# Hybrid decoder layer with 32 experts: buffers given back earlier, p @ ple_proj spread over the layer, returned rows on GpSimd's queue, sums a tile ahead

## The chip, the cores and the metric

The kernel runs on one core of one Trainium2 chip. The metric is the device time of one execution in microseconds (us), as the median of several runs. The engines in the text: TensorE (PE, with its weight loads PEld), VectorE (DVE), ScalarE (ACT), GpSimd (POOL) and SyncE (SP), of which SP here does nothing but issue DMAs. A queue is a list of DMAs that one engine issues in order: SP's runs as q1 in the profile, GpSimd's as q0.

## The reference

One decoder layer over 512 tokens of width 1024, all in float32. After the mixers (not touched here) come three steps:

```python
h = h + mix @ w_out                                        # out projection
h = h + hier_moe(rmsnorm(h, norm2_g), ...)                 # 4 groups x 8 experts, 2 experts per token
gate = sigmoid(rmsnorm(h, ple_norm_g) @ ple_gate_w + ple_gate_b)   # 1024 x 1024
e = p @ ple_proj_w                                         # 512 x 256 by 256 x 1024
h = h + gate * e
return rmsnorm(h, final_norm_g)
```

In `hier_moe` each token takes the best group and in it the best two of eight experts; an expert is `silu(t @ w_gate) * (t @ w_up)` (width 256) times its combine weight, and `@ w_down`. The reference computes all experts for all tokens; the kernel sends each expert only its own tokens.

## The kernel before, in words

**Experts by pairs.** The 32 experts run as 16 pairs. An expert has 64 slots for tokens, so a pair fills the 128 partitions. For pair i, `fetch` gathers the token rows from DRAM (xg, an indirect DMA by POOL, L934), `gather_T` transposes them on PE and scales them on DVE (two halves, L976 and L977), `gate_up` runs 32 matmuls (its records are at L988), ACT and DVE make hid (L993, L994), `down` transposes hid (L1010, L1011) and runs 8 matmuls dn (L1020, two records each, as all float32 matmuls here), ACT evicts dn (L1024), and POOL scatters the 128 rows to yd in DRAM (L1033). The rows of yd are sorted by token: two rows for each token, one for each of its experts. The last pair doesn't go through DRAM: `scatter` (L1041) multiplies its rows by one-hot matrices on PE and adds them to h1 on DVE (L1043).

**Weights and the ring.** The weights of the experts are 96 pieces of 1 MB, six for a pair: first k-half of both experts' gate and up, second k-half, then both downs (the order (0,3,1,4,2,5) in `load_units`, L689). Each lies in a buffer of 8 KB per partition, called unit. There are 20 units in a ring: `unit()` takes the first free one, `free()` puts it back. A load waits for the last reader of its unit's earlier contents, and for the landing of the load three ahead (AHEAD = 3). All these loads are on SP's queue, in the order in which the code is written; so are the gate's weights, the read-back of yd and the stores of half the result. SP waits for one load's conditions before it looks at the next.

**p @ ple_proj.** `ple_load` (L710, L711) loads pT, 0.5 MB, and pW, 1 MB, in pair 6, after gate/up(6). The product has 32 steps of one 128x256 matmul each (pe, L722); every fourth step is followed by an eviction on ACT (L725) into the tiles eo, two units taken in pair 7. The table PLE says how many steps run in pairs 8 to 14, all but one ahead of a pair's gate/up and one ahead of its down.

**The end.** After gate/up(14) the engines ACT and DVE, too, run in the written order, as PE and SP do throughout. After down(14) SP's queue has gate 0, then y0 (the read-back of the two yd rows of token tile 0, L1121, which waits for the last scatter), then gates 1 to 3, the bias row, y1 to y3 and the last norm's row. `add_y` adds the rows to h1 (L1117). The gate's weights are split into a high part (ACT, L1054) and a low part (DVE, L1057), eight splits of 128x1024. `turn` transposes h1 (L1176) and splits it; then come the products pg (L1197), three matmuls for each of eight k and each half, and `finish` with the last norm. `tail` goes through four token tiles; in the products of tile t it calls `sums(t + 1)` (add_y and scatter) and `prep(t + 1)` (turn). At the end a count tells whether an expert had more than 64 tokens; a branch that is not taken here would compute those.

**Order.** PE's and SP's instructions run in the order of the code, in the whole experts stage; ACT's and DVE's from pair 14 on.

## Time and profile before

| what | value |
|---|---|
| median of 3 runs | 562.01 us (561.25 to 562.83) |
| the profiled execution's own time | 562.7 us |
| its span | 560.9 us |
| mean granted TensorE clock | 0.97 |
| PE busy | 513.1 us, 91% of the span |
| DVE, ACT, POOL busy | 276.0, 209.8, 85.3 us |
| SP's queue q1 | 137.20 MB, 63.6% of the DMA engines' span |
| POOL's queue q0 | 7.95 MB, 3.8% |

The experts run from about 240 to 481 us of the span, the gate and the last norm from there to the end. Busy shares are means over stages with different limits, so the stages are to be read one by one: windows give each engine's busy time, the clock that the throttle granted to TensorE (1.00 is full speed) and how full the DMA engines were. A timeline row has start and length; in brackets stands how long the engine had been idle before, and what released it. A group of records can span waits that are shorter than the view's bound, so its length isn't always its busy time.

### The profile page before, as it was taken

What the parts mean: (1) busy time and instruction counts of PE and PEld (TensorE: products, weight loads), DVE (VectorE), ACT (ScalarE), POOL (GpSimd) and SP (SyncE); (2) the same over time, 40 slices, a digit from 0 to 9 for tenths busy, and PEclk for the clock granted to TensorE, in tenths of its full rate; (3) what the DMA queues carried; (4) which work ended last, traced back from release to release, by engine and by line L of the source; (5) the groups of instructions that cost most, each with busy time, mean ns of one, the idle gap of its engine ahead of it and who ended that gap; (6) DMA issues with size and microseconds to landing.
All of it is one profiled execution on the core that took longest, in us unless ns stands there. A gap on an engine that the chain in (4) does not pass through costs nothing.

```text
span 560.9 us, 7565 instructions
## 1 busy us (share of the span) xinstructions
PE 513.1 (91%) x2713; PEld 322.1 (57%) x2713; DVE 276.0 (49%) x727; ACT 209.8 (37%) x435; POOL 85.3 (15%) x122
## 2 busy tenths in 40 slices
PE   8899999999999999979999999099999999679992
PEld 5797886877997788934333333044434333347782
DVE  6663957757846666772422222022122112687774
ACT  7466765656857444211111111001111112363442
POOL 3301121311009400002111111001111100010000
PEclk9999999999999999998999999699999999899997
DMA  8882222300449579978999999999999999861111
GB/s 305 262 330 59 74 65 78 100 1 2 134 156 420 221 294 424 356 278 327 403 417 414 393 390 377 375 409 389 395 408 420 391 415 377 348 252 37 39 38 41
DMA packets 35641, 148.82 MB, mean 265 GB/s; under 512 B 6557, under 2 KB 13597, under 8 KB 22160
## 3 DMA queue, kind: packets, MB, share of 16 engines
q1 hardware_dynamic: 29984, 137.20, 63.6%
q0 software_dynamic: 4320, 7.95, 3.8%
q10 hardware_dynamic: 1296, 3.15, 1.4%
q8 instruction: 23, 0.38, 0.3%
q14 instruction: 18, 0.15, 0.1%
HBM read 139.61 MB, written 16.25 MB: 278 GB/s over the span
## 4 chain that ended last, share of the span: by engine, by line
PE 74%; DMA 10%; DVE 7%; ACT 5%; issue 2%; POOL 1%; SPq 0%; DVEq 0%; ACTq 0%; POOLq 0%
PE gu L988 17%; PE pj L232 9%; PE dn L1020 8%; PE po L78 8%; DMA unit<-in_w_exp_dram 5%; PE pj L255 5%; PE pg L1197 4%; PE z L255 4%; PE pe L722 3%; PE z L309 2%; DMA unit<-in_ple_proj_w_dram 2%; PE po L331 2%; DVE h L1117 2%; PE x L965 1%; DMA xg<-tnd,idx 1%
## 5 line engine op out<-in xcount | busy, mean ns | idle before, releaser
L988 PE MATMUL gu<-unit,xT 128*64 128x512 f32 x512 | 116.7, 597 | 0.0
L988 PEld LDWEIGHTS gu<-unit,xT 128*64 128x64 f32 x512 | 34.5, 136 | 62.3 <-issue 60.9
L1020 PE MATMUL dn<-unit,hidT 128*64 128x512 f32 x256 | 60.1, 612 | 1.0 <-ACT hidT L1011 0.5
L232 PE MATMUL pj<-xh,wp 128*128 128x512 f32 x176 | 51.2, 398 | 0.3 <-ACT wp L67 0.3
L1197 PE MATMUL pg<-unit 128*128 128x512 f32 (+1 forms) x216 | 49.4, 384 | 1.5 <-DVE unit L1057 1.5
L993 ACT ACTIVATE sg<-gu 128x256 f32<-128x256 f32 x16 | 6.1, 384 | 106.8 <-PE gu L988 106.8
L921 DVE COPY SL<-sl 128x10 f32<-128x10 f32 (+1 forms) x17 | 2.9, 168 | 85.0 <-PE sl L920 85.0
L1197 PEld LDWEIGHTS pg<-unit 128*128 128x128 f32 x216 | 37.9, 194 | 11.2 <-DVE unit L1057 3.4
L994 DVE SCALAR_TENSOR_TENSOR hid<-sg,wsl,gu 128x256 f32<-128x256 f32 x16 | 7.7, 480 | 74.4 <-ACT sg L993 74.4
L1033 POOL DMA_INDIRECT yd<-big,idy x15 | 15.1, 1009 | 150.4 <-ACT big L1024 150.4
L232 PEld LDWEIGHTS pj<-xh,wp 128*128 128x128 f32 x176 | 32.5, 188 | 8.1 <-ACT wp L67 1.2
L1020 PEld LDWEIGHTS dn<-unit,hidT 128*64 128x64 f32 x256 | 17.3, 140 | 33.6 <-issue 28.1
L1024 ACT ACTIVATE big<-dn 128x512 f32<-128x512 f32 x30 | 17.9, 597 | 49.6 <-PE dn L1020 49.6
L68 DVE TENSOR_TENSOR wp<-wraw,wp 128x768 fp32r<-128x768 f32 (+2 forms) x28 | 25.8, 928 | 13.6 <-ACT wp L67 13.4
L722 PE MATMUL pe<-unit,big 128*128 128x256 f32 x64 | 18.4, 420 | 13.4 <-DMA unit<-in_ple_proj_w_dram 13.4
L67 ACT ACTIVATE wp<-wraw 128x768 fp32r<-128x768 f32 (+2 forms) x28 | 22.8, 817 | 20.2 <-PE pj L232 9.8
L232 PE MATMUL pj<-xl,wp 128*128 128x512 f32 x88 | 29.4, 400 | 0.0
L78 PE MATMUL po<-wo,mx 128*128 128x512 f32 x96 | 25.6, 407 | 0.0
L255 PE MATMUL pj<-wp,xh 128*128 128x384 f32 x96 | 24.8, 351 | 0.0
L78 PE MATMUL po<-unit,mx 128*128 128x512 f32 x96 | 24.1, 400 | 0.0
L977 DVE TENSOR_TENSOR xT<-xt,g2c 128x512 f32<-128x512 f32 x30 | 20.6, 688 | 6.7 <-PE xt L976 6.7
L934 POOL DMA_INDIRECT xg<-tnd,idx x15 | 15.4, 1029 | 55.7 <-issue 35.7
(293 smaller groups left out, 878.8 us busy)
## 6 DMA issues: line engine op xcount, KB each, us to landing
unit<-in_w_exp_dram SPq DMA_DIRECT2D x96, 1024.0 KB, 9.2
wraw<-in_w_in_dram SPq DMA_DIRECT2D x20, 384.0 KB, 6.1
yd<-zero SPq DMA_DIRECT2D x4, 1024.0 KB
unit<-in_ple_gate_w_dram SPq DMA_DIRECT2D x4, 1024.0 KB
unit<-yd SPq DMA_DIRECT2D x4, 1024.0 KB, 4.8
wraw<-in_w_out_dram SPq DMA_DIRECT2D x8, 256.0 KB, 2.9
h<-in_x_dram SPq DMA_DIRECT2D x4, 512.0 KB, 4.1
unit<-in_w_out_dram SPq DMA_DIRECT2D x4, 512.0 KB, 7.9
```

The source lines that it names most:

```text
L67: nc.scalar.activation(h, src, AF.Copy)
L68: nc.vector.tensor_tensor(l, src, h.bitcast(F32), ALU.subtract)
L78: nc.tensor.matmul(p, a[k][:, ts_], K["wo"][k][:, b, hs], start=(n == 0), stop=(n == 3 * len(ks) - 1))
L232: PE.matmul(q, a[:, i * P:(i + 1) * P], b[k], start=(n == 0), stop=(n == 3 * KC - 1))
L255: PE.matmul(p[t][:, :W_IN[j]], a[k][:, t * P:(t + 1) * P], b, start=(n == 0), stop=(n == 3 * KC - 1))
L722: PE.matmul(p[:, c * 256:c * 256 + 256], pT[:, k * S + t * P:k * S + (t + 1) * P], pW[:, k, n:n + 256], start=(k == 0), stop=(k == 1))
L934: G.indirect_dma_start(out=xg[i % 2], out_offset=None, in_=tnd, in_offset=bass.IndirectOffsetOnAxis(ap=idx[:, i:i + 1], axis=0), bounds_ch ...
L977: V.tensor_tensor(xTs[i, hf], p.rearrange("p (a b) -> p a b", a=4), g2c[:, 4 * hf:4 * hf + 4, None].to_broadcast([P, 4, P]), ALU.mult)
L988: PE.matmul(gu[64 * e:64 * e + 64], xTs[i, k // 4][:, k % 4, 64 * e:64 * e + 64], w[e][k // 4][:, 512 * (k % 4):512 * (k % 4) + 512], star ...
L1020: PE.matmul(dn[64 * e:64 * e + 64], hT[:, f, 64 * e:64 * e + 64], w[e][2][:, 1024 * f + 512 * hf:1024 * f + 512 * hf + 512], start=(f == 0 ...
L1024: SC.activation(o[:, 512 * hf:512 * hf + 512], dn, AF.Copy)
L1197: PE.matmul(p, hT[t][:, a, ks], gw[k][:, b, hs], start=start and n == 0, stop=stop and n == len(ab) - 1)
```

## The change

- **Buffers.** In each pair the units of the first k-half (pieces 0 and 3) are put back into the ring at k == 3 of gate/up and the next loads are issued in the code there; before, all four of gate and up were put back after gate/up.
- **p @ ple_proj.** pT and pW are loaded after the first ten experts' loads that follow the router's bias. pW keeps a unit from then to the end. The steps run after gate/up of pair 0 (5), of each pair 1 to 13 (1), of 14 (2), and 4 + 4 + 4 in the end: after down(15), between `scatter` and `turn`, and after `turn`. The two tiles eo are taken in pairs 3 and 7; evictions wait in the list `kept` until their tile is there.
- **Queues.** The four read-backs y0 to y3 are issued by GpSimd (queue q0). SP's queue has the four gate loads and the two rows right behind the experts' last loads.
- **Gate.** Its weights are loaded as four pieces of 4 k by 512 columns and split by halves, 128x512: three splits of the first half ahead of add_y(0), the fourth after scatter, four after turn, then eight of the second half.
- **The end.** `sums(t + 2)` is called in the last products of tile t; before, `sums(t + 1)` in its first. The results of down(15) lie in one unit and no longer in the two big tiles. The stores are of 384 columns (ACT's queue) and 640 (SP's), before 512 and 512. The count of the tokens beyond 64 is written into pair 15 and ahead of the second half's splits.

SP's queue, from the router's bias to the end of the loads (w_exp: experts' weights; pT and ple_proj_w: the projection's inputs; yd: the scattered rows; ple_gate_w: the gate's weights), before:

```order
L702 DMA rb<-in_router_b_dram 128x36
L689 DMA unit<-in_w_exp_dram 128x2048 x47
L710 DMA big<-in_pT_dram 128x1024
L711 DMA unit<-in_ple_proj_w_dram 128x2048
L689 DMA unit<-in_w_exp_dram 128x2048 x40
L1050 DMA unit<-in_ple_gate_w_dram 128x2048
L1121 DMA unit<-yd 128x2x1024
L1050 DMA unit<-in_ple_gate_w_dram 128x2048 x3
L1151 DMA rows<-in_ple_gate_b_dram 128x1024
L1121 DMA unit<-yd 128x2x1024 x3
L1154 DMA rows<-in_final_norm_g_dram 128x1024
```

And now:

```order
L704 DMA rb<-in_router_b_dram 128x36
L691 DMA unit<-in_w_exp_dram 128x2048 x7
L712 DMA big<-in_pT_dram 128x1024
L713 DMA unit<-in_ple_proj_w_dram 128x2048
L691 DMA unit<-in_w_exp_dram 128x2048 x80
L1060 DMA unit<-in_ple_gate_w_dram 128x2048 x4
L1190 DMA rows<-in_ple_gate_b_dram 128x1024
L1191 DMA rows<-in_final_norm_g_dram 128x1024
```

pT and pW moved forty loads ahead, the four reads of yd left this queue, and the four gates follow the experts' weights without a break.

PE from down(15) on (ht and dn: down; sc: scatter; xt: turn; pg: the gate's products; pe: the projection's steps), before:

```order
L1010 MATMUL ht<-ident,hid 128x128 x2
L1020 MATMUL dn<-unit,hidT 64x512 x8
L1041 MATMUL sc<-big,xT 128x512 x4
L1176 MATMUL xt<-ident,h_0_1508 128x128 x8
L1197 MATMUL pg<-unit 128x512 x18
L1041 MATMUL sc<-big,xT 128x512 x4
L1197 MATMUL pg<-unit 128x512 x9
L1176 MATMUL xt<-ident,h_1_1509 128x128 x8
L1197 MATMUL pg<-unit 128x512 x27
L1041 MATMUL sc<-big,xT 128x512 x4
```

And now (om and pov: the count of tokens beyond 64):

```order
L1019 MATMUL ht<-ident,hid 128x128 x2
L1029 MATMUL dn<-unit,hidT 64x512 x8
L724 MATMUL pe<-unit,big 128x256 x4
L1051 MATMUL sc<-unit,xT 128x512 x4
L724 MATMUL pe<-unit,big 128x256 x4
L1213 MATMUL xt<-ident,h_0_1508 128x128 x8
L724 MATMUL pe<-unit,big 128x256 x4
L1129 LDWEIGHTS om
L1129 MATMUL pov<-cm,om 1x1
L1234 MATMUL pg<-unit 128x512 x18
L1051 MATMUL sc<-unit,xT 128x512 x4
L1234 MATMUL pg<-unit 128x512 x9
```

Twelve steps of pe moved into the end, four of them between scatter and turn and four between turn and the first products.

DVE from hid of pair 15 to the adds of tile 1 (h_0, h_1: token tiles of h1), before:

```order
L994 SCALAR_TENSOR_TENSOR hid<-sg,wsl,gu 128x256
L1117 TENSOR_TENSOR h_0_1508<-h_0_1508,unit 128x1024 x2
L1029 TENSOR_TENSOR big<-dn,big 128x512
L1057 SCALAR_TENSOR_TENSOR unit<-unit,g3c 128x1024
L1029 TENSOR_TENSOR big<-dn,big 128x512
L1043 TENSOR_TENSOR h_0_1508<-h_0_1508,sc 128x512 x2
L1057 SCALAR_TENSOR_TENSOR unit<-unit,g3c 128x1024
L1179 TENSOR_TENSOR unit<-xt,unit 128x512 x2
L1057 SCALAR_TENSOR_TENSOR unit<-unit,g3c 128x1024 x6
```

And now:

```order
L1003 SCALAR_TENSOR_TENSOR hid<-sg,wsl,gu 128x256
L1069 SCALAR_TENSOR_TENSOR unit<-unit,g3c 128x512 x3
L1158 TENSOR_TENSOR h_0_1508<-h_0_1508,unit 128x1024
L1039 TENSOR_TENSOR unit<-dn,unit 128x512
L1158 TENSOR_TENSOR h_0_1508<-h_0_1508,unit 128x1024
L1039 TENSOR_TENSOR unit<-dn,unit 128x512
L1053 TENSOR_TENSOR h_0_1508<-h_0_1508,sc 128x512 x2
L1069 SCALAR_TENSOR_TENSOR unit<-unit,g3c 128x512
L1216 TENSOR_TENSOR unit<-xt,unit 128x512 x2
L1069 SCALAR_TENSOR_TENSOR unit<-unit,g3c 128x512 x4
L1130 CAST on<-pov 1x1
L1069 SCALAR_TENSOR_TENSOR unit<-unit,g3c 128x512 x8
```

Three half splits moved ahead of the first add of y0, and the splits that stood between the adds became one half split behind them.

The diff (the count's formulas, the packing of the inputs on the host and the use of the count's tile in the branch that isn't taken are left out):

```diff
--- before.py
+++ after.py
@@ -27,7 +27,9 @@
 FILL = (8, 3, 0, 1, 0, 1, 0, 1, 0, 1, 1, 1, 4, 2, 2, 2, 9)
-PLE = {8: 5, 9: 5, 10: 5, 11: 5, 12: 4, 13: 4, 14: 4}
+PLE = (5, 1, 1, 1, 1, 1, 1, 1, 1, 1, 1, 1, 1, 1, 2)
+PLE_LAST = (4, 4, 4)
 AHEAD = 3
 NR, NL = 4, 9
@@ -703,7 +705,7 @@
-    pl_in, eo = [], []
+    pl_in, eo, kept = [], [], []
     def ple_load():
@@ -722,8 +724,15 @@
                               start=(k == 0), stop=(k == 1))
                     if c == k == 1:
-                        SC.activation(eo[t // 2][:, t % 2, hf * 512:hf * 512 + 512], p, AF.Copy)
+                        kept.append((t, hf, p))
+                        ple_out()
                     yield
+    def ple_out():
+        while kept and kept[0][0] // 2 < len(eo):
+            t, hf, p = kept.pop(0)
+            SC.activation(eo[t // 2][:, t % 2, hf * 512:hf * 512 + 512], p, AF.Copy)
     ple_left = ple_steps()
@@ -1023,8 +1032,9 @@
                 SC.activation(o[:, 512 * hf:512 * hf + 512], dn, AF.Copy)
                 continue
-            o2 = big(hf, F32R, (P, 2, 512))
-            oh, ol = o2[:, 0], o2[:, 1]
+            if hf == 0:
+                o2 = unit(F32R, [P, 4, 512])
+            oh, ol = o2[:, 2 * hf], o2[:, 2 * hf + 1]
             SC.activation(oh, dn, AF.Copy)
             V.tensor_tensor(ol, dn, oh.bitcast(F32), ALU.subtract)
@@ -1046,15 +1056,19 @@
     def gate_load(j):
-        gr.append(unit(F32, [P, 2, D]))
-        nc.sync.dma_start(gr[j], A["ple_gate_w"][:, 2 * j:2 * j + 2])
-    def gate_hi(k):
-        w = gw[k] = unit(F32R, [P, 2, D])
-        SC.activation(w[:, 0], gr[k // 2][:, k % 2], AF.Copy, scale=g3c[:, k:k + 1])
-    def gate_lo(k):
-        V.scalar_tensor_tensor(gw[k][:, 1], gr[k // 2][:, k % 2], g3c[:, k:k + 1], gw[k][:, 0].bitcast(F32), ALU.mult, ALU.subtract)
+        gr.append(unit(F32, [P, 4, 512]))
+        nc.sync.dma_start(gr[j], A["ple_gate_w"][j])
+    def split_gate(k, hf):
+        if hf == 0:
+            gw[k] = unit(F32R, [P, 2, D])
+        hs = slice(hf * 512, hf * 512 + 512)
+        raw, h, l = gr[2 * hf + k // 4][:, k % 4], gw[k][:, 0, hs], gw[k][:, 1, hs]
+        SC.activation(h, raw, AF.Copy, scale=g3c[:, k:k + 1])
+        V.scalar_tensor_tensor(l, raw, g3c[:, k:k + 1], h.bitcast(F32), ALU.mult, ALU.subtract)
+        if k % 4 == 3:
+            free(gr[2 * hf + k // 4])
     order.enter_context(tc.manual_schedule(engines={mybir.EngineType.PE}))
@@ -1079,6 +1093,7 @@
             gather_T(0, hf)
         one_hot(1, NT - 1)
+    ple_load()
     load_units()
@@ -1092,6 +1107,27 @@
         with tc.issue_after(K["exp"].ins):
             SC.preload_act_table_set("silu_and_others")
+    ov = {}
+    def beyond():
...
+        ov.update(cws=cws, om=om)
+    def count_beyond():
+        on = ov["on"] = mw.tile([1, 1], I32, name="on")
+        po = ps("pov", "xt")
+        PE.matmul(po[:1, :1], ov["om"], ones[:, :1], start=True, stop=True)
+        V.tensor_copy(on, po[:1, :1])
     def between(i):
@@ -1105,52 +1141,53 @@
             if k == (2 if i > 1 else 6):
                 slot_weights(i)
+            if k == 3:
+                free(slab[6 * i], slab[6 * i + 3])
+                load_units()
             if i == 15 and k == 5:
                 onehot_T(i)
+            if i == 15 and k == 6:
+                beyond()
         return go
     ys = []
-    def add_y(t):
-        for r in range(2):
+    def add_y(t, rs=(0, 1)):
+        for r in rs:
             V.tensor_tensor(h1[t], h1[t], ys[t][:, r], ALU.add)
     def load_y(t):
         ys.append(unit(F32, [P, 2, D]))
-        nc.sync.dma_start(ys[t], yd.rearrange("(r n) d -> n r d", r=2)[t * P:(t + 1) * P])
+        nc.gpsimd.dma_start(ys[t], yd.rearrange("(r n) d -> n r d", r=2)[t * P:(t + 1) * P])
     ends = ExitStack()
         if i == 14:
             ends.enter_context(tc.manual_schedule(engines={mybir.EngineType.Activation, mybir.EngineType.DVE}))
-        ple(PLE.get(i, 1) - 1)
         gate_up(i, between(i))
-        free(*(slab[6 * i + n] for n in (0, 3, 1, 4)))
+        free(slab[6 * i + 1], slab[6 * i + 4])
         if i == 15:
             break
-        if i == 6:
-            ple_load()
-        if i == 7:
-            eo += [unit(F32, [P, 2, D]) for _ in range(2)]
+        if i in (3, 7):
+            eo.append(unit(F32, [P, 2, D]))
+            ple_out()
         load_units()
+        if i == 0:
+            ple(PLE[0])
         gather_T(i + 1, 1)
-        if i in PLE:
-            ple(1)
+        if i > 0:
+            ple(PLE[i])
         down(i, lambda n: gather_T(i + 1, 0))
         free(slab[6 * i + 2], slab[6 * i + 5])
-        if i == 14:
-            free(pl_in[1])
         load_units()
         if i == 14:
-            gate_load(0)
-            load_y(0)
-            for j in range(1, 4):
+            for t in range(NT):
+                load_y(t)
+            for j in range(4):
                 gate_load(j)
             rows = mix.tile([P, 2, D], F32, name="rows", tag="m0")
             nc.sync.dma_start(rows[:, 0], bcast(A["ple_gate_b"]))
-            for t in range(1, NT):
-                load_y(t)
             nc.sync.dma_start(rows[:, 1], bcast(A["final_norm_g"]))
@@ -1212,10 +1249,10 @@
             ms = mean_sq(ms, m[:, j:j + 1])
         r = rsqrt_cols(nc, mw, ms, 1, "rsl", K)
-        SC.activation(ot[:, :512], ot[:, :512], AF.Copy, scale=r)
-        nc.scalar.dma_start(out[t * P:(t + 1) * P, :512], ot[:, :512])
-        V.tensor_scalar(ot[:, 512:], ot[:, 512:], r, None, ALU.mult)
-        nc.sync.dma_start(out[t * P:(t + 1) * P, 512:], ot[:, 512:])
+        SC.activation(ot[:, :384], ot[:, :384], AF.Copy, scale=r)
+        nc.scalar.dma_start(out[t * P:(t + 1) * P, :384], ot[:, :384])
+        V.tensor_scalar(ot[:, 384:], ot[:, 384:], r, None, ALU.mult)
+        nc.sync.dma_start(out[t * P:(t + 1) * P, 384:], ot[:, 384:])
     def last(t, at={}):
@@ -1226,12 +1263,16 @@
         finish(t, [(hf, c, n, ps("pg", "pg")[:, :n]) for hf, c, n in pieces], products)
-    def tail(sums=lambda t: None):
+    def tail(sums=None):
         for t in range(NT):
             at = {}
             if t + 1 < NT:
-                at[0, 6 if t == 0 else 2], at[1, 1] = lambda: sums(t + 1), lambda: prep(t + 1)
+                at[1, 1] = lambda: prep(t + 1)
+            if sums and t == 0:
+                at[0, 6] = lambda: sums(1)
+            if sums and t + 2 < NT:
+                at[1, 5] = lambda: sums(t + 2)
             last(t, at)
@@ -1239,29 +1280,32 @@
             scatter(2 * t + hf)
-    def split_gate(k):
-        gate_hi(k)
-        gate_lo(k)
-        if k % 2:
-            free(gr[k // 2])
     def behind_down(n):
         if n == 0:
-            add_y(0)
+            for k in range(3):
+                split_gate(k, 0)
+            add_y(0, (0,))
         if n == 1:
-            split_gate(0)
+            add_y(0, (1,))
     down(15, behind_down)
+    ple(PLE_LAST[0])
     for hf in range(2):
         scatter(hf)
-    split_gate(1)
+    split_gate(3, 0)
+    ple(PLE_LAST[1])
     lo = [turn(0, hf) for hf in range(2)]
+    ple(PLE_LAST[2])
+    free(pl_in[1])
     for f in lo:
         f()
-    for k in range(2, KC):
-        split_gate(k)
-    ov_slots = ring[:4]
-    junk, h3s = (unit(F32, shape, slot) for shape, slot in zip(([P, 2, 512], [P, 4, 512]), ring[4:]))
+    for k in range(4, KC):
+        split_gate(k, 0)
+    count_beyond()
+    for k in range(KC):
+        split_gate(k, 1)
+    ov_slots = ring[:3]
+    junk, h3s = (unit(F32, shape, slot) for shape, slot in zip(([P, 2, 512], [P, 4, 512]), ring[3:]))
     SC.preload_act_table_set("sigmoid_and_others")
     rms(0)
     tail(sums)
```

## Rows read from the trace of the kernel before

**Rows 1.** The page's span in 40 slices of 14 us: the mean busy share of the 16 DMA engines in tenths, and what they moved.

```profile
DMA  8882222300449579978999999999999999861111
GB/s 305 262 330 59 74 65 78 100 1 2 134 156 420 221 294 424 356 278 327 403 417 414 393 390 377 375 409 389 395 408 420 391 415 377 348 252 37 39 38 41
```

**Rows 2.** Windows by stage. Columns: from and to, length, then busy time and count of PE, PEld, DVE, ACT and POOL, then the granted TensorE clock, the DMA share and GB/s.

```profile
265.00:350.00 85.00, 80.88 (x412) 29.57 (x408) 24.59 (x103) 13.14 (x27) 12.16 (x12) 1.00 1.00 398
350.00:364.00 14.00, 0.64 (x5) 0.16 (x1) 0.00 (x0) 0.60 (x1) 1.01 (x1) 0.62 0.99 375
364.00:475.00 111.00, 110.30 (x528) 44.92 (x530) 22.26 (x87) 18.72 (x37) 13.13 (x13) 0.99 1.01 405
475.00:503.00 28.00, 18.18 (x69) 9.36 (x65) 20.62 (x26) 14.09 (x19) 1.48 (x1) 0.94 0.78 309
```

**Rows 3.** Timeline of PE and of SP's queue around 350 to 372 us: start, length, engine, line, operation.

```profile
352.46 0.42 SPq L711 DMA_DIRECT2D unit<-in_ple_proj_w_dram  x1
...
363.88 3.54 PE L722 MATMUL pe<-unit,big 128*128 128x256 f32 x8 [13.36 <-DMA unit<-in_ple_proj_w_dram]
```

**Rows 4.** What SP's queue waited for between 230 and 480 us: us in total, times, longest.

```profile
SPq L689 <- DMA unit<-in_w_exp_dram: 185.9, 74, 5.8
SPq L689 <- PE gu L988: 15.6, 7, 8.2
...
SPq L689 <- PE dn L1020: 5.8, 3, 5.3
```

**Rows 5.** The chain of work that ended last, between 290 and 400 us: start, length, what.

```profile
295.43 3.65 PE dn L1020 x16
...
308.29 3.65 PE dn L1020 x16
...
380.42 1.93 PE pe L722 x8
```

**Rows 6.** Timeline of SP's queue, of POOL and of PE from 462 to 479 us.

```profile
462.15 5.32 SPq L689 DMA_DIRECT2D unit<-in_w_exp_dram  x3
...
469.29 0.98 POOL L1033 DMA_INDIRECT yd<-big,idy  x1 [13.12 <-ACT big L1024]
...
477.07 0.38 SPq L1121 DMA_DIRECT2D unit<-yd  x1
477.50 1.69 SPq L1050 DMA_DIRECT2D unit<-in_ple_gate_w_dram  x3
...
477.69 3.65 PE L1020 MATMUL dn<-unit,hidT 128*64 128x512 f32 x16 [0.47 <-ACT hidT L1011]
```

**Rows 7.** DMA issues, of 470 to 490 us (y) and of 299 to 346 us (xg and yd, indirect, 0.5 MB each): queue, count, KB where the view has it, median us from issue to landing.

```profile
unit<-yd SPq DMA_DIRECT2D x4, 1024.0 KB, 4.8
...
yd<-big,idy POOLq DMA_INDIRECT x4, 8.6
xg<-tnd,idx POOLq DMA_INDIRECT x4, 10.4
```

**Rows 8.** Timeline of DVE and PE in the end: the first adds of y0, tile 0's transposes, the first products, and the transposes of tiles 1 to 3.

```profile
481.86 2.49 DVE L1117 TENSOR_TENSOR h<-h,unit 128x1024 f32<-128x1024 f32 x2 [5.13 <-DMA unit<-yd]
...
487.39 2.10 PE L1176 MATMUL xt<-ident,h 128*128 128x128 f32 x8
489.19 2.52 PE L1197 MATMUL pg<-unit 128*128 128x512 f32 x7
...
502.44 1.25 PE L1176 MATMUL xt<-ident,h 128*128 128x128 f32 x8 [2.51 <-DVE h L1043]
...
518.44 1.26 PE L1176 MATMUL xt<-ident,h 128*128 128x128 f32 x8 [1.07 <-DVE h L1043]
...
533.07 1.26 PE L1176 MATMUL xt<-ident,h 128*128 128x128 f32 x8 [1.36 <-DVE h L1043]
```

**Rows 9.** Timeline of SP's queue and of PE in pair 0's gate/up.

```profile
245.52 0.82 SPq L689 DMA_DIRECT2D unit<-in_w_exp_dram  x2
...
248.63 1.08 PE L988 MATMUL gu<-unit,xT 128*64 128x512 f32 x4
```

**Rows 10.** Windows of 5 us at the start of the experts and in the end; columns as in rows 2.

```profile
240.00:245.00 5.00, 5.00 (x34) 2.63 (x35) 3.59 (x19) 1.24 (x7) 0.40 (x1) 1.00 0.57 238
...
255.00:260.00 5.00, 5.00 (x18) 1.41 (x16) 0.32 (x1) 0.71 (x2) 0.87 (x1) 0.72 0.77 315
...
485.00:490.00 5.00, 3.94 (x13) 2.51 (x13) 4.71 (x6) 1.07 (x2) 0.00 (x0) 0.66 0.98 384
```

**Rows 11.** DMA queues from 316.5 to 320 us, when both had work: packets, MB, share of the 16 engines.

```profile
q1 hardware_dynamic: 134, 0.97, 68.0%
q0 software_dynamic: 181, 0.41, 29.7%
```

**Rows 12.** Timeline of POOL around 313 us.

```profile
312.89 1.02 POOL L1033 DMA_INDIRECT yd<-big,idy  x1 [10.12 <-ACT big L1024]
314.61 1.01 POOL L934 DMA_INDIRECT xg<-tnd,idx  x1 [0.71 <-issue]
```

**Rows 13.** Groups of instructions by line and shape, 240 us to the end: count, busy us, mean ns of one, idle before.

```profile
L1057 DVE SCALAR_TENSOR_TENSOR unit<-unit,g3c 128x1024 fp32r<-128x1024 f32 x8 | 9.8, 1281 | 0.3 <-ACT unit L1054 0.3
...
L725 ACT ACTIVATE unit<-pe 128x512 f32<-128x512 f32 x8 | 4.8, 598 | 19.7 <-PE pe L722 19.7
...
L1029 DVE TENSOR_TENSOR big<-dn,big 128x512 fp32r<-128x512 f32 x2 | 1.4, 684 | 0.0
```

More of the change, by code (lines that the diff above doesn't have):

```diff
@@ L1094, in first @@
             SC.preload_act_table_set("silu_and_others")
+    ov = {}
+    def beyond():
+        cws = mw.tile([P, NT, 32], F32, name="cws", tag="Dm")
+        cwe = cws.rearrange("p t (i e) -> p t i e", e=2)
+        V.tensor_tensor(cwe, Rt[:, :, :, 0:2], Rt[:, :, :, 2:4], ALU.add)
+        V.tensor_tensor(cwe, cwe, Rt[:, :, :, 4:6], ALU.add)
+        V.scalar_tensor_tensor(cws, posA, CAP - 1024.0, cws, ALU.is_ge, ALU.mult)
+        om = mw.tile([P, 1], BF, name="om")
+        omx = small("omx", 1)
+        V.tensor_reduce(omx, cws, mybir.AxisListType.XY, ALU.max)
+        V.tensor_scalar(om, omx, 0.0, None, ALU.is_gt)
+        ov.update(cws=cws, om=om)
[4 more added lines that the diff above has]
+        V.tensor_copy(on, po[:1, :1])
     def between(i):
@@ L1269, in ffn @@
     order.close()
-    cws = mw.tile([P, NT, 32], F32, name="cws", tag="Dm")
-    cwe = cws.rearrange("p t (i e) -> p t i e", e=2)
-    V.tensor_tensor(cwe, Rt[:, :, :, 0:2], Rt[:, :, :, 2:4], ALU.add)
-    V.tensor_tensor(cwe, cwe, Rt[:, :, :, 4:6], ALU.add)
-    V.scalar_tensor_tensor(cws, posA, CAP - 1024.0, cws, ALU.is_ge, ALU.mult)
-    om, on = mw.tile([P, 1], BF, name="om"), mw.tile([1, 1], I32, name="on")
-    omx = small("omx", 1)
-    V.tensor_reduce(omx, cws, mybir.AxisListType.XY, ALU.max)
-    V.tensor_scalar(om, omx, 0.0, None, ALU.is_gt)
-    po = ps("pov", "xt")
-    PE.matmul(po[:1, :1], om, ones[:, :1], start=True, stop=True)
-    V.tensor_copy(on, po[:1, :1])
-    n_over = nc.values_load(on[0:1, 0:1], min_val=0, max_val=P)
+    n_over = nc.values_load(ov["on"][0:1, 0:1], min_val=0, max_val=P)
     def overflow():
@@ L1289, in overflow @@
         for t in range(NT):
-            nc.sync.dma_start(ocd.rearrange("e p t -> p e t")[:, :, t], cws[:, t])
+            nc.sync.dma_start(ocd.rearrange("e p t -> p e t")[:, :, t], ov["cws"][:, t])
         with tc.For_i(0, 32, 1) as e:
@@ L1402, in pack @@
     d["ple_proj_w"] = np.ascontiguousarray(g["ple_proj_w"][0].reshape(2, P, D).transpose(1, 0, 2))
-    d["ple_gate_w"] = np.ascontiguousarray(g["ple_gate_w"][0].reshape(KC, P, D).transpose(1, 0, 2))
+    d["ple_gate_w"] = np.ascontiguousarray(g["ple_gate_w"][0].reshape(2, 4, P, 2, 512).transpose(3, 0, 2, 1, 4)).reshape(4, P, 4, 512)
     d["ple_gate_b"] = g["ple_gate_b"][0]
```

## The prediction

> **What bounds the kernel now.** I read the page's slices first. The DMA line of [rows 1] is at 9 from the experts' start to near their end, and low in the last sixth, where TensorE (PE) has the work. The windows by stage [rows 2] sharpen this: from 265 to 475 us the DMA share is 0.99 to 1.01 at 375 to 405 GB/s. So the experts stage is bound by its transfers. TensorE looks bound too (110.30 of 111.00 us busy after 364), but only because it stood still before that: one wait of 13.36 us at 363.88 for the projection's weights pW [rows 3]. Their load was issued only at 352.46, behind expert weights on the same queue, and took 11.4 us until PE went on. While TensorE stood, the transfers went on at 375 GB/s [rows 2]: nothing was lost on the side that binds. The third view, the SP queue's waits [rows 4], says the same: 74 waits of an expert's load for an earlier load's landing, 185.9 us in sum, against 15.6 and 5.8 us of waits for TensorE to be done with a buffer.
>
> TensorE's own need is smaller than the transfers'. A pair of experts goes from one dn to the next in 308.29 - 295.43 = 12.86 us, and with 4 steps of pe 1.93 more [rows 5]. Without the stall TensorE would be ready for pair 15 some 13 us sooner, while the last weights, issued up to 467.5 at the transfers' pace [rows 6], land when they do now.
>
> The end is a chain: yd(14) is scattered at 469.29, row tile y0 is read back at 477.07 and lands 4.8 us later [rows 6, 7], DVE starts its adds at 481.86, the gate's first product runs at 489.19 and h1[1] is ready for PE at 502.44 [rows 8]. From 481.86 to 502.44 DVE is nearly never idle (20.62 us busy in 475 to 503, [rows 2]). From there to 550 PE runs with two waits, 1.07 and 1.36 us [rows 8].
>
> **The change, part by part.** The sum is made against the profiled execution, 562.7 us; the median of the runs shown is 562.0, so 0.7 comes off at the end.
>
> *Buffers given back half-way (free at k == 3).* In pair 0 the load of the next pair's weights already goes out at 245.52, while gate/up(0) still issues its matmuls at 248.63 [rows 9]: the semaphore is that of the last reader, not of the line where the buffer is freed. The queue waits for landings anyway [rows 4]. 0.
>
> *pT and pW early, steps spread.* The stall of 13.36 goes. What is late next is the last weight. Its landing is set by the bytes and the ring: pT and pW are 1.57 MB, 3.9 us at 405 GB/s, and they move from the saturated stretch to one where the DMA share is 0.57 to 0.77 [rows 10]. That is a gain of up to 3. Against it, pW holds one of the 20 buffers from the start, one 1 MB load (2.6 us) less of lead, and the output tiles eo take theirs at pairs 3 and 7 instead of both at 7. I take -1 for the landing of the last weights and so for dn(15), now at 477.69 [rows 6]; bounds -3 and +3. Five steps stand on PE right after gate/up(0), with pW in the queue only ten loads after the first experts'; should PE wait there, up to 4 us go into a slack of 13. The cover of the moved steps is that slack; if it were gone, 20 steps in the pairs would cost nothing more than now, since 32 stand there before.
>
> *Row tiles y by GpSimd's queue, gates ahead on SP.* Now the SP queue holds gates 1 to 3 back until y0 is issued, so y0 has the engines almost alone: 4.8 us for 1.05 MB. After, four gates and two rows, 5.2 MB, stand on SP's queue (q1) ahead, and y0 goes out on q0 when yd(14) has landed. When both queues are full, q0 moved 0.41 MB in 3.5 us against 0.97 MB of q1, 29.7% of the engines' time [rows 11]. At that pace 1.05 MB take 9.0 us; with the 2.2 us that y0 needs now over 1.05 MB at 405 GB/s it is 11.2. The second way to the same number: yd issued at 312.89 and xg at 314.61, together also 1.05 MB, were all landed 10.4 after the second issue, 12.1 after the first [rows 7, 12]. I take 11.7, so +6.9 against 4.8. Bounds: 0 (it lands as if alone) and +9 (all 5.2 MB first: 13 us, less 4.8, plus a little). Under it stand on POOL no other waiters but the three later tiles; under the first add on DVE stands everything of the end. The Trainium skill ("DMA: Bandwidth & Descriptors", "Queues, rings and completion order") says that each DMA engine takes the queue rows that have work in turn, a packet at a time, and (same page, "Issuing engines are not separate DMA queues") that another issuing engine saves only the sequencer's time: both speak against this edit. By taking turns two full queues would share evenly: an estimate from that page is 1.05 MB at half of 405 GB/s, 5.2 us and 2.2 more, y0 after 7.4 and the sum at 564.3; the trace's 29.7% is less than a half, so the row decides.
>
> *From y0 to h1[1].* Eight splits of 1.28 become sixteen halves of about 0.69 (0.684 for the same form of add, [rows 13]), three of them ahead of y0's arrival: 13 x 0.69 = 9.0 against 10.2, so -1.2. On PE 4 steps now stand between scatter(1) and the turn's transposes: 1.93 at full clock, 3.54 at half [rows 3, 5], less the 0.85 by which the transposes take longer there now than for the next tile (2.10 against 1.25, [rows 8]): +1.1 to +2.7. PE has waited for y0 until then, and the clock after such a wait is low now too (0.66 in 485 to 490, 0.62 in the stall, [rows 10, 2]), so I take +2.4. The third 4 steps put their eviction (0.6, [rows 13]) on ACT ahead of splits 4 to 7, which wait for PE's 1.93: +1.2. Sum +2.4; bounds -1 (the splits' gain alone) and +5 (both at half clock).
>
> *Sums a tile ahead.* The two waits, 1.07 and 1.36 [rows 8], can go, but DVE has the same adds to do in the same stretch: -1.5, bounds -2.4 and +1. *384/640 and the overflow count moved*: a little less on ACT ahead of the last store, -0.2.
>
> Sum: -1 + 6.9 + 2.4 - 1.5 - 0.2 = +6.6, so 569.3 for a profiled execution and 568.6 for the median.
>
> **Rivals.**
> 1. *Faster (the other side): the transfers have room.* The mechanism: a full DMA share counts packets waiting in flight as busy, and once PE no longer stops at pair 7 buffers come free evenly and the queue runs at the 420 GB/s of its better slices [rows 1] and not at 375 to 405. Over 210 us that is 5%, 10 us, all of it inside the 13.36 that PE gives back. Then dn(15) comes some 10 us earlier; y0 is late as above: 568.6 less 9 to 13 gives 556 to 560, middle 557. It decides from 7 us of gain in the weights' landing on. For it: slices of 409 to 420 exist. Against: in 265 to 350, with no stall, the rate was 398 [rows 2], and 74 of the waits are for landings.
> 2. *y0 lands promptly.* GpSimd's ring is not held back, y0 lands in 5 to 7 us, be it that GpSimd's queue gets its even half: the term of 6.9 falls to between 0 and 2.5, middle 1, 563. For it: xg and yd are scattered rows, y is not, so their pace may be a bad measure. Against: xg and yd move 4 KB rows at the share of [rows 11], and now two such sets need 12.
> 3. *Worse: the slack turns into waits with a low clock.* If PE, now ahead, waits for weights in pairs 13 to 15, its clock falls as it did in the stall (0.62, [rows 2]), and what comes after the last landing runs at 1.83 times (3.54 against 1.93): dn(15) 3.65 takes 6.7, the second half of gate/up(15), as many matmuls of that size, 3.0 more, together +6, 575. For it: PE must wait somewhere, 13 us of it. The Trainium skill ("TensorE: Matmul & The Clock Gate", "HAM oscillation") tells the same of matmul loops that wait for DMA between bursts; the drop to 0.62 in the stall agrees. By it the sum gets the 6 us. Against: waits spread over many pairs are short, and the clock was 0.99 where PE had none.
>
> **How the numbers follow.** Forecast case 0.54; rival 1 0.15; rival 2 0.14; rival 3 0.17. The forecast's own range is 564 to 573, from its terms' bounds taken together at about half their ends. The range 557 to 577 takes in rival 2 and nearly all of rival 3, and the middle of rival 1 lies at its edge; outside it I leave 0.1 of rival 1 and some 0.05 of rival 3. About 0.3%, 1.7 us, is what a measurement can tell from no change here. Faster: rival 1 and a part of rival 2, 0.16. Same: half of rival 2, 0.07. Slower: the rest, 0.77.
>
> **What would show it.** In the profile of the changed kernel: no wait for pW of over 4 us; PE's waits for expert weights in pairs 10 to 15, 10 us or more in sum; the last weights' landing and dn(15) within 3 us of now (right for the first term), or 8 or more earlier (rival 1); y0 from issue to landing 10 to 13 us (right), about 5 (rival 2); pe steps after dn(15) at 1.9 or 3.5 per 4; the waits before the turns of tiles 2 and 3 gone; clock of the last pairs about 1.0 (right) or 0.6 to 0.8 (rival 3). The prediction is wrong if dn(15) moves by over 5 us either way or y0 isn't late.

## The result, and the profile after

The changed kernel takes 565.68 us (median of 9 runs, 564.26 to 566.76) against 561.25 for the kernel before (9 runs, 559.01 to 562.83): ratio 1.0086, 95% interval 1.0065 to 1.0107. It is slower, by 4.4 us in the medians. The forecast was 568.6, slower, with the range 557 to 577.

The profiled executions, 562.7 and 564.66 us, lie 1.5 above and 1.0 below their medians, so they differ by 2.0 only: less than half of the 4.4 of the medians. Within them the way to the end falls into four stretches, each from one row to the next:

| stretch | before | after | measured | forecast |
|---|---|---|---|---|
| y0 is issued at | 477.07 | 469.37 | -7.7 | -1 |
| from there to the first add of y0 | 4.8 | 12.3 | +7.5 | +6.9 |
| from there to the transposes of tile 1 | 20.6 | 24.6 | +4.0 | +2.4 |
| from there to the end of the span | 58.5 | 56.6 | -1.8 | -1.7 |

The first stretch is read from the page's DMA slices, the windows by stage and the list of PE's waits (answers to [rows 1 to 3]). The page's slices:

```profile
DMA  9881222300549589989999999999999999900111
GB/s 312 272 315 55 75 80 75 86 1 2 146 164 421 198 322 421 334 343 397 411 414 418 392 381 376 374 399 381 391 392 419 419 412 418 401 6 0 39 47 69
```

Windows, columns as in rows 2:

```profile
240.00:245.00 5.00, 5.00 (x33) 2.34 (x33) 3.88 (x19) 1.61 (x7) 0.77 (x1) 1.00 0.90 378
...
255.00:260.00 5.00, 5.00 (x29) 1.62 (x26) 1.26 (x8) 1.19 (x2) 1.19 (x2) 1.00 1.01 387
...
350.00:364.00 14.00, 13.90 (x72) 5.16 (x70) 4.50 (x23) 1.96 (x4) 2.50 (x3) 1.00 1.00 387
364.00:475.00 111.00, 96.08 (x420) 35.37 (x418) 18.16 (x65) 14.86 (x31) 14.08 (x15) 1.00 1.00 401
```

What PE waited for from 240 us on: us in total, times, longest.

```profile
PE gu L997 <- DMA unit<-in_w_exp_dram: 12.2, 11, 2.0
PE xt L1213 <- DVE h L1053: 6.6, 1, 6.6
PE sc L1051 <- DVE unit L1039: 5.9, 2, 5.4
```

The stall at 350 to 364 is gone (13.90 of 14.00 busy), and the early hole in the transfers is filled: 378 and 387 GB/s where rows 10 have 238 and 315. In 240 to 265 us the queues moved 9.08 MB instead of 7.32. PE now waits for weights, 11 times, 12.2 us in sum, never over 2.0, and from 364 to 475 the clock stays at 1.00. In the kernel before, the same list has no wait for an expert's weight at all; its longest entry is the stall:

```profile
PE pe L722 <- DMA unit<-in_ple_proj_w_dram: 13.4, 1, 13.4
```

The end, timeline of the engines (answers to [rows 6, 8]):

```profile
455.49 8.39 SPq L691 DMA_DIRECT2D unit<-in_w_exp_dram  x4
463.93 2.09 SPq L1060 DMA_DIRECT2D unit<-in_ple_gate_w_dram  x4
...
460.97 1.00 POOL L1043 DMA_INDIRECT yd<-big,idy  x1 [15.51 <-ACT big L1033]
469.37 2.94 POOL L1162 DMA_DIRECT2D unit<-yd  x4 [7.40 <-PE pD L1010]
...
472.32 3.65 PE L1029 MATMUL dn<-unit,hidT 128*64 128x512 f32 x16 [0.47 <-ACT hidT L1020]
...
481.66 1.23 DVE L1158 TENSOR_TENSOR h<-h,unit 128x1024 f32<-128x1024 f32 x1 [4.56 <-DMA unit<-yd]
...
485.87 3.73 PE L724 MATMUL pe<-unit,big 128*128 128x256 f32 x8
489.43 1.04 PE L1213 MATMUL xt<-ident,h 128*128 128x128 f32 x8
490.30 1.89 PE L724 MATMUL pe<-unit,big 128*128 128x256 f32 x8
...
492.73 7.46 ACT L1068 ACTIVATE unit<-unit,g3c 128x512 fp32r<-128x512 f32 x12
...
506.26 1.97 PE L1213 MATMUL xt<-ident,h 128*128 128x128 f32 x8 [6.63 <-DVE h L1053]
```

The scatter yd(14) goes out at 460.97 instead of 469.29, the last expert load ends its issue at 463.88 instead of 467.47, dn(15) starts at 472.32 instead of 477.69. All of that is early. y0 isn't: issued 7.7 sooner, it takes 12.3 us from its issue to the first add, and its first add starts at 481.66, where it started before (481.86). PE stands still for 5.4 us ahead of scatter's second matmul; then eight records of pe (four steps, two records each) take 3.73 us, eight more 1.89, and ACT starts its twelve half splits at 492.73. The queues while y0 is under way (packets, MB, share of the 16 engines), from 470 to 476 and then from 476 to 482 us:

```profile
q1 hardware_dynamic: 291, 2.12, 84.6%
q0 software_dynamic: 98, 0.40, 16.4%
```

```profile
q1 hardware_dynamic: 227, 1.66, 66.8%
q0 software_dynamic: 223, 0.85, 35.1%
```

Up to 473.4 us, 4.0 after the issue, the same view (DMA queues by window) has no packet of q0 at all. From 476 on the two queues move the same number of packets, but a packet of q0 holds 3.8 KB on average and one of q1 7.3, so q0 gets a third of the bytes.

### The profile page after: what moved, and what is told of

Its sections match the earlier page's. It is cut to its first block, busy times and chain, and to the rows that moved or that the text cites. A ratio compares the mean times of both kernels' runs of the same rounds, so it can differ in the third digit from the quotient of the medians.

```text
span 562.9 us, 7588 instructions
## 1 busy us (share of the span) xinstructions
PE 517.0 (92%) x2713; PEld 325.5 (58%) x2713; DVE 276.7 (49%) x735; ACT 210.6 (37%) x443; POOL 90.3 (16%) x126
## 5 line engine op out<-in xcount | busy, mean ns | idle before, releaser
L997 PE MATMUL gu<-unit,xT 128*64 128x512 f32 x512 | 127.6, 598 | 12.4 <-DMA unit<-in_w_exp_dram 12.2
L997 PEld LDWEIGHTS gu<-unit,xT 128*64 128x64 f32 x512 | 37.1, 136 | 84.0 <-issue 59.0
L1234 PE MATMUL pg<-unit 128*128 128x512 f32 (+1 forms) x216 | 47.4, 376 | 1.1 <-ACT unit L1215 1.1
L1029 PEld LDWEIGHTS dn<-unit,hidT 128*64 128x64 f32 x256 | 19.1, 136 | 33.1 <-issue 24.5
L70 DVE TENSOR_TENSOR wp<-wraw,wp 128x768 fp32r<-128x768 f32 (+2 forms) x28 | 25.8, 928 | 13.7 <-ACT wp L69 13.4
L986 DVE TENSOR_TENSOR xT<-xt,g2c 128x512 f32<-128x512 f32 x30 | 20.6, 688 | 11.8 <-PE xt L985 11.7
L985 PEld LDWEIGHTS xt<-ident,xg 128*128 128x128 f32 x120 | 13.4, 140 | 11.5 <-issue 11.4
```

What stands on the lines that cost most here:

```text
L70: nc.vector.tensor_tensor(l, src, h.bitcast(F32), ALU.subtract)
L986: V.tensor_tensor(xTs[i, hf], p.rearrange("p (a b) -> p a b", a=4), g2c[:, 4 * hf:4 * hf + 4, None].to_broadcast([P, 4, P]), ALU.mult)
L997: PE.matmul(gu[64 * e:64 * e + 64], xTs[i, k // 4][:, k % 4, 64 * e:64 * e + 64], w[e][k // 4][:, 512 * (k % 4):512 * (k % 4) + 512], star ...
L1029: PE.matmul(dn[64 * e:64 * e + 64], hT[:, f, 64 * e:64 * e + 64], w[e][2][:, 1024 * f + 512 * hf:1024 * f + 512 * hf + 512], start=(f == 0 ...
L1234: PE.matmul(p, hT[t][:, a, ks], gw[k][:, b, hs], start=start and n == 0, stop=stop and n == len(ab) - 1)
```

## The experiments

Twelve kernels ran. Each is compared with the kernel before on the same chip (medians 561.0, 560.9 and 560.7 in the three sittings). The ratios are those of the record and not quotients of the medians (for e4 these give 0.992).

| kernel | median us | ratio to before | 95% interval |
|---|---|---|---|
| e1 read-backs on SP's queue | 557.69 | 0.9922 | 0.9893 to 0.9951 |
| e2 steps in the pairs | 560.39 | 0.9990 | 0.9966 to 1.0014 |
| e3 both | 557.04 | 0.9921 | 0.9893 to 0.9950 |
| e9 gates held back | 559.27 | 0.9955 | 0.9933 to 0.9976 |
| e4 before, with early pT and pW | 556.39 | 0.9892 | 0.9854 to 0.9930 |
| e5 no release half-way | 564.72 | 1.0053 | 1.0026 to 1.0079 |
| e6 sums late | 566.97 | 1.0086 | 1.0056 to 1.0117 |
| e8 no steps in pair 0 | 565.52 | 1.0078 | 1.0048 to 1.0107 |
| e7 before, with read-backs on POOL | 569.20 | 1.0146 | 1.0117 to 1.0176 |
| e13 e4 with read-backs on POOL | 562.37 | 1.0015 | 0.9984 to 1.0046 |
| e10 e4 with sums ahead | 555.12 | 0.9898 | 0.9870 to 0.9926 |
| e11 e10 with steps in PE's wait | 558.35 | 0.9951 | 0.9916 to 0.9986 |

My theory after the result: the early pT and pW gain, since yd(14) comes 8 us sooner; the read-backs behind the gates and the steps in the end give all of it back and more. The rival: the end is bound by DVE and ACT whatever y0 does.

**e1, read-backs on SP's queue in the old order.**

```diff
-        nc.gpsimd.dma_start(ys[t], ...)
+        nc.sync.dma_start(ys[t], ...)
...
-            for t in range(NT):
-                load_y(t)
-            for j in range(4):
-                gate_load(j)
+            gate_load(0)
+            load_y(0)
+            for j in range(1, 4):
+                gate_load(j)
...
+            for t in range(1, NT):
+                load_y(t)
```

> The changed kernel, with the four read-backs of yd on SP's queue in the order of the kernel before (gate 0, y0, gates 1 to 3, bias row, y1 to y3, last row). Theory: y0 lands late because 5.2 MB of gates and rows stand ahead on the other queue while yd(14) itself lands 8 us sooner than before (468.8). Then y0 is issued at about 469, lands behind gate 0 at 476 to 477 in place of 481.66, and all that follows moves by -5, with up to -1.8 more because PE stands still for less time ahead of the 8 records of pe (3.73 at a lower clock): 559 to 561 in place of 565.7. Rival (the end is bound by DVE and ACT, and y0 has little to do with it): first products at 490 to 492 as now, total 564 to 566.

557.69, 8 less than the changed kernel: the theory, and more than the 559 to 561 that it gave. Timeline of SP, DVE and PE:

```profile
469.07 0.38 SPq L1162 DMA_DIRECT2D unit<-yd  x1
...
477.23 1.22 DVE L1158 TENSOR_TENSOR h<-h,unit 128x1024 f32<-128x1024 f32 x1
...
481.43 1.99 PE L724 MATMUL pe<-unit,big 128*128 128x256 f32 x8
483.26 1.04 PE L1215 MATMUL xt<-ident,h 128*128 128x128 f32 x8
484.13 1.89 PE L724 MATMUL pe<-unit,big 128*128 128x256 f32 x8
...
486.05 4.42 PE L1236 MATMUL pg<-unit 128*128 128x512 f32 x18
```

The first add is 4.4 sooner. The pe steps take 1.99 instead of 3.73; ahead of them PE waited for 0.8 and 1.0 us and not for 5.4.

**e2, all steps of pe in the pairs; e3, that and e1.**

```diff
-PLE = (5, 1, 1, 1, 1, 1, 1, 1, 1, 1, 1, 1, 1, 1, 2)
-PLE_LAST = (4, 4, 4)
+PLE = (5, 1, 1, 3, 3, 3, 3, 2, 2, 2, 2, 2, 1, 1, 1)
+PLE_LAST = (0, 0, 0)
```

> The changed kernel with all 32 steps of pe in the pairs (5, 1, 1, 3, 3, 3, 3, 2, 2, 2, 2, 2, 1, 1, 1) and none in the end. Theory: the 4 us that the way from y0 to the transposes of tile 1 got longer are the pe steps on PE (3.73 + 1.89) and their evictions on ACT ahead of the splits; PE's 12.2 us of waits for weights in the late pairs take up the 12 steps (5.6 us). y0 stays at 481.7 (within 1), transposes of tile 1 at 501.5 to 503 in place of 506.26, total -3 to -4.5: 561 to 562.7. Rival (the half splits on ACT, 12 x 0.62 in a row and then the table load, set that way): transposes of tile 1 at 505 to 506.5, total within 1 of 565.7.

> Both edits: read-backs on SP's queue in the old order, and all steps of pe in the pairs. Theory: the two costs add, -5 and -3 to -4.5: 556 to 558, below both kernels. Rival: with y0 at 476 to 477 the end waits for the gates' splits or for dn(15), and only one of the two gains shows: 560 to 562.

In e2 the way from the first add to the transposes of tile 1 is 20.4 us instead of 24.6, and the total 560.39, 5.3 less than the changed kernel and a little below the 561 to 562.7 of the theory. The way of 20.4 bears the theory out: the steps cost 4.2, and PE's waits in the pairs take them up. But y0, which was to stay at 481.7 within 1, was added from 480.03 on, 1.6 sooner; why was not tried, and in e5, with its steps in the end, the first add is at 479.82. With both edits it is 557.04, only 0.65 less than e1, and the two medians lie within each other's runs: the gains don't add. Timeline of DVE and PE in e3:

```profile
476.81 1.22 DVE L1158 TENSOR_TENSOR h<-h,unit 128x1024 f32<-128x1024 f32 x1
...
484.61 6.41 PE L1236 MATMUL pg<-unit 128*128 128x512 f32 x18
...
497.18 1.25 PE L1215 MATMUL xt<-ident,h 128*128 128x128 f32 x8 [3.16 <-DVE h L1053]
```

Windows of e1, then of e3, columns as in rows 2:

```profile
480.00:485.00 5.00, 4.08 (x22) 3.40 (x23) 3.15 (x6) 1.54 (x3) 0.00 (x0) 1.00 1.01 412
```

```profile
480.00:485.00 5.00, 3.17 (x11) 2.19 (x12) 4.23 (x7) 2.45 (x5) 0.00 (x0) 0.50 1.01 410
```

From the first add to the transposes of tile 1 e3 needs 20.4 us and e1, with the steps, 22.9 (to 500.10). So the steps cost 4.2 us in the changed kernel and 2.5 in e1, where PE has hardly stood still ahead of them and its clock is at 1.00. In e3 the clock is at 0.50 and the first 18 records of the products take 6.41 instead of 4.42, but DVE, busy for 4.23 of the 5 us, seems to set the pace there: e3's way is the shorter one all the same. From the transposes of tile 1 to the end e3 needs 57.1 and e1 56.2; where these 0.9 go was not tried.

**e9, read-backs on GpSimd's queue, but gate 1 waits for y0's landing.**

```diff
+        if j == 1:
+            tc.add_manual_dep(g, y_in[0].name, ...)   # g: gate 1's load, y_in[0]: y0's
```

> The changed kernel with the read-backs on GpSimd's queue as they are, but gate 1 and all that follows on SP's queue waits until y0 has landed. It tells the queue from what stands ahead: if y0 is late because the two queues share the engines, it lands 4 to 7 us after its issue at about 469.4 (the last two expert loads and gate 0 still run), at 474 to 477, and the total is 559 to 562. Rival (GpSimd's queue is slow by itself): y0 lands 10 to 12 after its issue, at 480 to 482, and as the gates come later the total is 566 to 570.

GpSimd's queue isn't slow by itself: y0, issued at 471.29, is added from 477.93 on, 6.6 us later. What makes it 12.3 in the changed kernel is what stands ahead on the other queue. Both parts of the wait shrink: q0's first packet comes 1.7 us after the issue (4.0 in the changed kernel), and from 474 on q0 has nearly all of the engines' time. Timeline of POOL and DVE:

```profile
471.29 2.93 POOL L1164 DMA_DIRECT2D unit<-yd  x4 [7.78 <-PE gu L997]
...
477.93 1.22 DVE L1160 TENSOR_TENSOR h<-h,unit 128x1024 f32<-128x1024 f32 x1
```

**e4, the kernel before with early pT and pW alone**, all steps in the pairs as in e2.

```diff
+    ple_load()                    # no longer in pair 6
     load_units()                  # behind gather_T(0)
...
-        if i == 7:
-            eo += [...]
+        if i in (3, 7):
+            eo.append(...)
```

> The kernel before with one part of the change: pT and pW loaded after the first ten experts' loads, eo taken in pairs 3 and 7, all 32 steps of pe in the pairs (5, 1, 1, 3, 3, 3, 3, 2, 2, 2, 2, 2, 1, 1, 1); read-backs, gates, splits and sums as before. Theory: this part alone is what makes the way to the last pairs shorter (yd(14) landed 8 us and dn(15) 5 us sooner in the changed kernel). y0 is issued at about 469 on SP's queue, lands behind gate 0 at 476 to 477 in place of 481.83, and the end of 79 us follows: 555.5 to 557.5 against 561.2. Rival (the gain needs the other parts, above all buffers given back half-way): yd(14) lands no more than 3 us sooner, 558.5 to 561.

556.39, as the theory had it: one part of the change, by itself, makes the kernel faster, by 4.5 us in the medians (ratio 0.9892). y0 is issued at 468.35 on SP's queue and added from 475.91 on; from there to the transposes of tile 1 it is 20.6 us, as before.

**e5, buffers of gate and up given back together; e6, sums late; e8, no steps in pair 0.**

```diff
# e5
-            if k == 3:
-                free(slab[6 * i], slab[6 * i + 3])
-                load_units()
...
-        free(slab[6 * i + 1], slab[6 * i + 4])
+        free(*(slab[6 * i + n] for n in (0, 3, 1, 4)))
# e6
-            if sums and t == 0:
-                at[0, 6] = lambda: sums(1)
-            if sums and t + 2 < NT:
-                at[1, 5] = lambda: sums(t + 2)
+                if sums:
+                    at[0, 6 if t == 0 else 2] = lambda: sums(t + 1)
# e8
-PLE = (5, 1, 1, ...)
+PLE = (0, 6, 1, ...)
```

> The changed kernel with all four buffers of gate and up given back after gate/up, as before. Theory (a load waits for the last reader, not for the line that frees its buffer): loads go out at the same times, total within 1 us of 565.7. Rival (the queue gets to the next loads sooner): the load after slab 20 goes out 1 to 4 us later in pair 0, the stage ends 2 to 3 later, 567.5 to 569.

> The changed kernel with the adds and scatters of tile t + 1 in the first products of tile t, as before. Theory: PE's waits of 1.1 and 1.4 ahead of the transposes of tiles 2 and 3 are back: 567 to 568.2. Rival (DVE does the same adds in the same stretch, the wait only moves): within 0.7 of 565.7.

> The changed kernel without the five steps of pe after gate/up(0) (they run in pair 1, six in all). In the changed kernel these steps fill PE's wait for the gathered rows xg(1), and the clock in 250 to 260 us is 1.00 where it was 0.60 and 0.72 before; dn(0) takes 3.65 in place of 5.29. Theory: the wait of about 1.9 us and the low clock are back, dn(0) takes 5.2 to 5.3, pair 1 starts 2 to 2.5 later, buffers come free as much later, and since the transfers bind the stage, its end moves by 1 to 2.5: 566.5 to 568. Rival (PE's 12 us of waits in the late pairs take it all up): dn(0) slow, but yd(14) and the total within 0.7 of now.

e5: 564.72, 1.0 less than the changed kernel with overlapping intervals: the release half-way gains nothing. e6: 566.97, 1.3 more in the medians, but the ratio to the kernel before is that of the changed kernel, 1.0086, so the totals don't tell the two apart. The rows do: PE's waits are back, 1.23 and 1.47, and in the profiled executions the way from the transposes of tile 1 to the end is 57.56 us (505.74 to the end of the span, 563.3) instead of 56.64. e8: 565.52, no change, the rival. Of its theory the wait came back, the low clock didn't. Rows of e6, then of e8:

```profile
521.50 1.26 PE L1213 MATMUL xt<-ident,h 128*128 128x128 f32 x8 [1.23 <-DVE h L1053]
...
536.20 1.25 PE L1213 MATMUL xt<-ident,h 128*128 128x128 f32 x8 [1.47 <-DVE h L1053]
```

```profile
253.79 0.63 PE L985 MATMUL xt<-ident,xg 128*128 128x128 f32 x4 [1.41 <-DMA xg<-tnd,idx]
...
255.11 3.65 PE L1029 MATMUL dn<-unit,hidT 128*64 128x512 f32 x16
```

**e7, the kernel before with the read-backs on GpSimd's queue; e13, e4 with them.** The edit is that of e1 backwards.

> The kernel before with one part of the change: the read-backs on GpSimd's queue and the four gates and rows on SP's queue right behind the experts' weights. Theory: y0 goes out at 477 as now, shares the engines with 5.2 MB and lands 11 to 12.5 us later, at 488 to 489.5 in place of 481.8; the clock falls while PE waits: total 567 to 570. Rival (by 477 a good part of the gates has already landed, so the share is small): y0 at 483 to 485, total 563 to 565.

> The early pT and pW with all steps in the pairs (556.4 by itself) and the read-backs on GpSimd's queue, nothing else. Theory: y0 goes out at about 469 and lands at 480.5 to 482 in place of 476.5, PE stands still for 8 us ahead of it and its clock falls: 561 to 563.5, so these two parts alone make what the whole change gains and loses up to about 3. Rival (what the changed kernel loses is mostly in its splits, steps and stores): 557 to 559.

e7: 8.5 us slower than before in the medians, 5.4 in the spans of the profiled executions, of which y0's first add carries 5.0. That add is at 486.82 (theory 488 to 489.5), 9.0 after y0's issue at 477.83 and not 11 to 12.5: q0 has no packet up to 481.2, 3.4 after the issue, but the gates have mostly landed by then, and from 482 on q0 has 86% of the engines' time and more. e13: 562.37, 6.0 more than e4: with these two parts alone nearly all of e4's gain is lost again. y0 is issued at 471.43 and added from 483.30 on, 11.9 later. Timeline of e7, of e13:

```profile
486.82 2.49 DVE L1117 TENSOR_TENSOR h<-h,unit 128x1024 f32<-128x1024 f32 x2 [10.54 <-DMA unit<-yd]
```

```profile
483.30 2.48 DVE L1125 TENSOR_TENSOR h<-h,unit 128x1024 f32<-128x1024 f32 x2 [10.14 <-DMA unit<-yd]
```

**e10, e4 with the sums a tile ahead; e11, that with eight steps of pe behind down(15).**

```diff
# e10: e6 backwards, on e4
# e11, against e10
-PLE = (5, 1, 1, 3, 3, 3, 3, 2, 2, 2, 2, 2, 1, 1, 1)
+PLE = (5, 1, 1, 3, 3, 3, 3, 1, 1, 1, 1, 1, 0, 0, 0)
...
     down(15, behind_down)
+    ple(8)
...
```

> The early pT and pW with all steps in the pairs, and the sums a tile ahead, all else as before. Theory: the two parts that gain add up: PE's waits of 1.2 each ahead of the transposes of tiles 2 and 3 go, 554.5 to 555.5 against 556.4; since both edits of the read-backs and the steps undone in the changed kernel gave 557.0, this would put 1.5 to 2.5 us of loss on the half splits and what goes with them. Rival (the adds only wait elsewhere): 556 to 557.

> The same with the last eight of the 32 steps of pe between down(15) and scatter, where PE stands still for y0 (3.4 us). Theory: they cost nothing there and hold the clock at 1.00: transposes of tile 0 in 1.0 in place of 2.1 and the first products in half the time; as DVE sets the pace after that, 0.3 to 1 us less than without: 553.8 to 555.2. Rival (they run past the wait and delay scatter and the splits): 0.5 to 1.5 more.

e10 takes 555.12, 1.3 less than e4 (the intervals overlap; in the profiled executions the way from the transposes of tile 1 to the end is 56.3 us instead of 59.0), and has the lowest median of this study, 1.0% below the kernel before and 10.6 us below the changed one. e11 is a miss, 558.35 (555.45 to 561.66). ACT's row, timeline:

```profile
477.86 3.72 PE L722 MATMUL pe<-unit,big 128*128 128x256 f32 x16
...
481.62 0.60 ACT L1035 ACTIVATE big<-dn 128x512 fp32r<-128x512 f32 x1 [7.39 <-PE pe L722]
```

The first eviction of dn, whose matmuls were through at 477.9, starts only behind the last step of pe. It may be that one wait stands for both evictions and for what PE does in between; that isn't shown. Nor is the eviction all of the miss. Of the 4.2 us between the profiled executions of e10 and e11, 2.2 are there at y0's first add already (476.12 and 478.28), since e11's y0 was issued later and took longer; 2.0 come between that add and the transposes of tile 1 (20.6 and 22.6 us), where the late eviction lies; none come after.

## Why the prediction was right, and where its sum was not

The way (slower) and the reason for it (y0 held up by the gates) were right; the size 568.6 was 2.9 above, and two terms of the sum were mis-sized.

- **"I take -1 for the landing of the last weights and so for dn(15)"**: this step failed. At y0's issue it was -7.7 and at dn(15) -5.4 (472.32), both beyond the bound of -3, and the second beyond the 5 us that the prediction itself had named as a sign that it is wrong. I let both hang on the last weights. But in the kernel before PE's list of waits has none for an expert's weight, so behind its stall of 13.4 us PE itself set the time of pairs 14 and 15, though the transfers were full. y0 waits for yd(14), that is for pair 14, and there PE, no longer behind, came 8.3 us sooner; at dn(15) PE's new waits for weights had left 5.4 of it. Only the issue of the last load is bound by the transfers, and that came 3.6 sooner, also beyond the bound: of the estimated 3.9 us for the bytes of pT and pW, moved into the hole of rows 10, nearly all were gained. e4 shows what this part is worth by itself, 4.5 us in the medians.
- **"Row tiles y by GpSimd's queue ... I take 11.7"**: 12.3 measured. The cause was right: e9 (6.6 us with the gates held) and e1 show it. That the size came out is in part luck, since two errors offset. From 476 to 482 us q0 moved 0.85 MB, at which 1.05 MB take 7.4 us (an estimate) and not 9.0; so the rest of the 12.3 is 4.9 us and not the 2.2 taken from SP's queue, most of it the 4.0 before q0's first packet. The Trainium skill ("DMA: Bandwidth & Descriptors", "Queues, rings and completion order") says that the engines take the queue rows in turn, packet by packet. The trace agrees: 223 packets of q0 against 227 of q1 in these 6 us. What failed was the step from equal turns to equal bytes, the half that gave 7.4 us in all: q0's packets held about half as much as q1's.
- **"From y0 to h1[1] ... +2.4"**: +4.0, inside its bounds. The steps of pe cost as in the working, 3.73 at the low clock and 1.89. But the half splits gained 0.2 (20.4 us in e2 and e3, 20.6 in before, e4 and e7) and not 1.2; what took the rest was not tried by itself, and neither were the half splits.
- **"Sums a tile ahead ... -1.5" and the -0.2**: right, -1.8 in the profiled executions; of that the sums give 0.9 by e6's rows, but 2.7 by those of e4 and e10. The stores and the moved count were not tried by themselves.
- **The buffers half-way, 0**: right (e5).
- **Rival 1** needed the last weights 7 us sooner; they came 3.6, and the rate from 364 to 475 us was 401 GB/s (405 before) and not 420. **Rival 2** fell with y0's 12.3. **Rival 3**: PE did wait in the last pairs, 12.2 us, but in eleven pieces of up to 2.0, and the clock stayed at 1.00.

By the terms the profiled executions give -7.7 + 7.5 + 4.0 - 1.8 = +2.0, the medians +4.4. The kernel before's execution is a long one, the changed one's a short one; what differs between runs of one kernel is left open. So it is in part luck that the forecast of 568.6 lies within 3 us of the median: the first term alone was 6.7 too high, the other three together 2.1 too low, and the two profiled executions, against which the sum was made, differ by 2.0 and not by 6.6.

## What to carry to other kernels

Before a bulk load is put ahead on one queue, ask which small read on another queue falls into its time: here up to 5.2 MB of prefetch turned a read of 4.8 us into one of 12, and it was on the path while the prefetch was not. A queue that "blocks" behind a wait can be what gives the late, urgent transfer the engines to itself. When a stall on one engine is removed in a stage bound by transfers, look for who hangs on that engine and not on the last transfer; here 8.3 of the 13.4 us came out there, and 3.6 at the last transfer.
